# Gate's 4th and 5th inputs in other buffers, eight up pieces ahead of the MLP's first sums, and the last half tile in two pieces

## Chip, cores and metric

The kernel runs on one core of a Trainium2 chip. The metric is the device time of one execution in microseconds (us). Engines are named as in the profile: PE (TensorE, matrix products and transposes), DVE (VectorE), ACT (ScalarE), POOL (GpSimd) and SP (SyncE, which only issues transfers, DMAs, here). SBUF is the memory on the chip that all of them share, PSUM the banks that products are summed in.

## The reference

One layer of a bidirectional encoder on a sequence of 2048 rows of 1024 numbers (float32): attention with two groups of heads, an MLP, and a gated embedding, each behind a norm and added to the row.

```python
u = rmsnorm(h, g_pre_mix); proj = u @ w_in
mix = concat([rmsnorm(windowed_gqa_sink(...)), rmsnorm(dilated_mixture(...))]) @ w_o
h = h + rmsnorm(mix, g_post_mix)
v_ = rmsnorm(h, g_pre_mlp)
a = relu(v_ @ w_up)                       # w_up: 1024 x 4096
h = h + rmsnorm((a * a) @ w_down, g_post_mlp)
gate = sigmoid(h @ w_ple_gate + b_ple_gate)
h = h + rmsnorm(gate * (p @ w_ple_proj), g_post_ple)
```

## The kernel before, in words

Every float32 product is made of three products of parts: each operand is split into a high part (a rounded copy, made by ACT) and a low part (the difference, made by DVE), and hi times hi, lo times hi and hi times lo are summed in PSUM. A "piece" below is such a group of three products for one slice of 128 of the summed index, with 512 columns each. The names end in h and l for the two parts: `uph`, `upl` of the up weights, `dnh`, `dnl` of the down weights, `ah`, `al` of the MLP's inner values, `hh_`, `hl_` of a gate tile.

The stages follow one another: projection, attention, out projection and norms (32 half tiles, counted by `s`, up to 1258 us of the profile), MLP (1258 to 2614 us), gate (2614 us to the end).

**MLP.** The loop over `n` has 32 rounds (two halves of the rows, 16 groups of columns of the up weights each). A round makes the sums of one group, in 28 "downs" of three products each (`down`, L1284, products at L1293, into PSUM tiles `psd` and `psy`), and beside them the up products of the next round, 32 pieces (`up`, L1265). One of these 32 pieces stands behind most of the downs. The down products are arranged so that seven are made where eight would be needed, of sums and differences of operands, which POOL makes (`combo`, L1137, results `tmp`). Steps that other engines must do are put into a queue by `later(dt, step)`; `tick()`, called once behind each down, issues those that are due. So the order on PE, ACT, DVE, POOL and SP in this stage is written out by the code, and each engine runs its own instructions in that order.

The first round is special: its first down needs `al` of the first inner values, which stand behind the last norms of the stage before on DVE (`norm2`, L1099). `FIRST` is a table that puts some of the first round's steps at other ticks. In the first round of each half, `piece` copies sums of `psd` and `psy` by ACT, into the accumulators `acc` (L1296), and for the second of the seven products into `dmp` (L1299), which POOL then adds; a `psy` tile is free for the next down when its copy has been made. There are two `psy` tiles.

**Up weights.** `up_weights(ahead)` (L1143) issues the load of one weight group into `upraw` (L1147, one buffer), and queues four steps: high part of its first half `ahead` ticks later (ACT, L1153), low part (DVE, L1156), and the same of the second half. The buffer is free when the last low part is made. In the out-projection stage it is called at `s` of 8, 15 and 28.

**Gate.** Sixteen tiles `t` of 128 rows, `d_item(t)` in three steps: load `h` and `pl` (`s1`, L1498 and L1500), transpose `h` on PE (L146) and split it (`s2`, L128 and L129), and products, sigmoid, norm and store (`s3`, from L1515 on). For t of 0 to 2 the transposes and splits, and for 0 and 1 the products, are made in the MLP's last round, from `heads`. The loads `h2` share three buffers, and the `h` of a tile is added to its result at the very end, so the buffer of tile 0 is free for tile 3 only when tile 0's result is made. SP's order here comes from a scheduler.

**Last tile.** The last tile's two halves of 512 columns are worked off in turn: bias (L1527), sigmoid (L1528), times `pl` (L1529), square sum (L1531, ACT), times `gp` (L1532); then the two square sums are added (`mt`, L1540), 1 over the root is made by POOL (`rstd_of`), and the result is written (L1543).

Of the kernel before, what the change touches and what calls it, by code (L numbers as in the profile page):

```python
# [12 lines left out]
F32 = mybir.dt.float32  # L13
# [6 lines left out]
D = 1024  # L20
# [39 lines left out]
def layer(ctx, tc, a, out):  # L60
# [354 lines left out]
    def tick():  # L415
        while clock[0] in todo:
            for fn in todo.pop(clock[0]):
                fn()
        clock[0] += 1
# [698 lines left out]
    E_ = 32  # L1118
    FIRST = {6: 17, 14: 21, 15: 22, 16: 23, 17: 24, 18: 21, 20: 23, 24: 25}
    halves_ = []  # L1120
    for n, t in enumerate(c_order):
# [241 lines left out]
    for s in range(E_):  # L1363
        n, hf = s // 2, s % 2
        if hf == 0:
            c_norm(n)
        halves_[n](hf)
        if s in (8, 15, 28):
            up_weights(6 if s == 28 else 3)
        if s == E_ - 1:  # L1370
            prepare(0, x, xs, ws, (-17, FIRST))
        if s >= 19:
            next(u0)
            done += 1
        tick()
    wopx.close()
    stage.close()
    with ExitStack() as st:
# [24 lines left out]
        def gate_load():  # L1403
            for t in range(3):
                h = ru.tile([128, D], F32, name="h0", tag="upraw") if t == 2 else vr.tile([128, D], F32, name="h0", tag="vraw")
                sp.dma_start(h, hd[128 * t : 128 * t + 128, :])
                heads[t] = [h]

        def gate_turn(t, g):
# [28 lines left out]
        for n in range(32):  # L1438
# [19 lines left out]
            if n < 31:  # L1458
                x, xs, ws = {}, [], []
                work = (xs, ws)  # L1460
                prepare((n + 1) % 16, x, xs, ws)
                u = up((n + 1) // 16, (n + 1) % 16, x)
            if n == 30:
                later(20, gate_load)
            if n == 31:
                u = gate_first()
            done = 0
            for m in range(28):
                next(d)
                if n == 31 and m < 4:  # L1470
                    gate_turn(m // 2, m % 2)
                while u and done < ((m + 1) * 32 // 28 if n < 31 else (m - 3) * 32 // 24):
                    next(u)
                    done += 1
                if u and m == 27:
                    run(u)
                feed_up()
                tick()
# [14 lines left out]
        def d_item(t):  # L1493
            box = {}

            def s1():
                h = hp.tile([128, D], F32, name="h2", tag="h2", bufs=3)
                sp.dma_start(h, hd[128 * t : 128 * t + 128, :])  # L1498
                pl = hp.tile([128, D], F32, name="pl", tag="pl", bufs=3)
# [15 lines left out]
            def s3():  # L1515
                y = hp.tile([128, D], F32, name="y", tag="y")
                if t == 15:
                    ms = sml.tile([128, 2], F32, name="ms2", tag="ms2")
                for hf in range(2):
# [3 lines left out]
                    else:  # L1523
                        ps = psm.tile([128, 512], F32, name="psm", tag="psm")
                        mm3(ps, 8, lambda k: box["hh"][:, k, :], lambda k: box["hl"][:, k, :],
                            lambda k: vt[hf][0][:, k, :], lambda k: vt[hf][1][:, k, :])
                    dve.tensor_add(y[:, cs], ps, bb[:, cs])  # L1527
                    act.activation(y[:, cs], y[:, cs], AF.Sigmoid)  # L1528
                    dve.tensor_mul(y[:, cs], y[:, cs], box["pl"][:, cs])  # L1529
                    if t == 15:  # L1530
                        act.activation(box["pl"][:, cs], y[:, cs], AF.Square, scale=1.0 / 32.0, accum_out=ms[:, hf : hf + 1])  # L1531
                        dve.tensor_mul(y[:, cs], y[:, cs], gp[:, cs])  # L1532
                if t < 15:
# [4 lines left out]
                else:  # L1538
                    mt = sml.tile([128, 1], F32, name="mt", tag="mt")
                    dve.tensor_add(mt, ms[:, 0:1], ms[:, 1:2])  # L1540
                    r = rstd_of(mt)
                    for cs in (slice(0, 512), slice(512, 1024)):
# [40 lines left out]
```

## Time and profile before

| what | before |
|---|---|
| three runs | 2798.73, 2804.01, 2804.07 us; median 2804.01 |
| the profiled execution | 2803.37 us |
| its span, first to last instruction | 2801.6 us |
| granted TensorE clock, mean over the span | 0.987 of full speed |
| PE busy | 2716.6 us, 97% of the span |

The time of an execution is 1.77 us more than its span. PE is busy in nearly all slices of the profile, so what can be won lies in the stretches where PE waits, or runs at a lower granted clock. [...]

### The profile page before, as it was taken

To read this page: it belongs to the slowest core of one execution; us is meant where nothing else is said; L and a number is where in the kernel's file an instruction comes from. 1 tells how busy PE (TensorE), PEld (TensorE's weight loads), DVE (VectorE), ACT (ScalarE), POOL (GpSimd) and SP (SyncE) were. 2 spreads that over 40 slices of the span, in tenths; PEclk is the share of its full clock that TensorE was granted. 3 is DMA by queue.
4 is the path that set the end of the run, shared out by engine and by line. 5 is a ranking of instruction groups with operands and counts; after the bars stand their busy time and mean duration, and the time that the engine had idled before them with its cause. 6 is when DMAs were issued, how large, how long until landed. Compare 5 with 4: busy or idle time off the path is not lost.

```text
span 2801.6 us, 38950 instructions
## 1 busy us (share of the span) xinstructions
PE 2716.6 (97%) x13952; PEld 2129.1 (76%) x13952; DVE 1755.1 (63%) x3420; ACT 1273.3 (45%) x2944; POOL 933.1 (33%) x950
## 2 busy tenths in 40 slices
PE   7999999999999999999999999999999999999898
PEld 6878866666677677777888888888888888887687
DVE  4210244456666563776787787777677778786665
ACT  4321345566565554555444444445444444443332
POOL 3000033331322211435345345345345345344220
PEclk9999999999999899999999999999999999999999
DMA  6232252325534325773222122235223223333553
GB/s 178 83 116 81 97 158 74 112 78 141 134 85 127 72 95 169 268 249 98 79 72 75 61 76 72 68 124 195 102 69 104 91 73 112 102 94 150 195 197 104
DMA packets 247873, 324.39 MB, mean 116 GB/s; under 512 B 19904, under 2 KB 175552, under 8 KB 245280
## 3 DMA queue, kind: packets, MB, share of 16 engines
q1 hardware_dynamic: 220544, 281.73, 32.0%
q10 hardware_dynamic: 27136, 40.18, 4.0%
q8 instruction: 110, 1.80, 0.3%
q14 instruction: 83, 0.68, 0.1%
HBM read 227.16 MB, written 102.04 MB: 118 GB/s over the span
## 4 chain that ended last, share of the span: by engine, by line
PE 53%; DVE 1%; ACT 1%; issue 0%; DMA 0%; POOL 0%; DVEq 0%; POOLq 0%; ACTq 0%
PE psd L1293 13%; PE psy L1293 10%; PE psu L174 9%; PE psu L175 9%; PE psu L173 8%; PE psm L137 2%; PE psm L138 2%; PE psm L139 2%; PE pst L146 0%; ACT dmp L1341 0%; ACT y L1528 0%; DMA out_dram<-y 0%; DVE dnl L1132 0%; DVE y L1536 0%; DVE hl L1419 0%
## 5 line engine op out<-in xcount | busy, mean ns | idle before, releaser
L1302 DVE TENSOR_TENSOR acc<-acc,psd 128x512 f32<-128x512 f32 x488 | 332.6, 685 | 190.7 <-PE psd L1293 185.2
L174 PE MATMUL psu<-vt,uph 128*128 128x512 f32 x1024 | 407.4, 398 | 0.0
L175 PE MATMUL psu<-vt,upl 128*128 128x512 f32 x1024 | 404.7, 395 | 0.0
L173 PE MATMUL psu<-vt,uph 128*128 128x512 f32 x1024 | 401.8, 392 | 0.0
L1137 POOL TENSOR_TENSOR tmp<-rl 128x512 f32<-128x512 f32 x64 | 84.2, 1316 | 673.8 <-ACT rl L1281 673.2
L768 ACT ACTIVATE e<-e,tm 128x256 f32<-128x256 f32 (+1 forms) x384 | 176.6, 461 | 120.3 <-DVE tm L765 118.7
L174 PEld LDWEIGHTS psu<-vt,uph 128*128 128x128 f32 x1024 | 192.3, 188 | 48.1
L173 PEld LDWEIGHTS psu<-vt,uph 128*128 128x128 f32 x1024 | 192.6, 188 | 45.0
L175 PEld LDWEIGHTS psu<-vt,upl 128*128 128x128 f32 x1024 | 192.1, 188 | 43.6
L1302 DVE TENSOR_TENSOR acc<-acc,psy 128x512 f32<-128x512 f32 x248 | 170.1, 686 | 86.3 <-PE psy L1293 76.3
L1280 ACT ACTIVATE rl<-psu 128x512 f32<-128x512 f32 x128 | 76.4, 597 | 305.7 <-PE psu L175 305.7
L1300 POOL TENSOR_TENSOR acc<-acc,dmp 128x512 f32<-128x512 f32 x128 | 191.3, 1506 | 57.9 <-DVE al L1132 31.5
L1293 PE MATMUL psd<-dnh,al 128*128 128x512 f32 x512 | 204.0, 398 | 4.8 <-DVE al L1132 4.8
L133 DVE SCALAR_TENSOR_TENSOR wc<-wraw,pre_mix_t,wc 128x128 fp32r<-128x128 f32 x176 | 58.4, 379 | 234.9 <-ACT wc L132 234.9
L1293 PE MATMUL psd<-dnh,ah 128*128 128x512 f32 x512 | 202.1, 395 | 1.9 <-ACT ah L1131 1.9
L1293 PE MATMUL psd<-dnl,ah 128*128 128x512 f32 x512 | 201.4, 393 | 0.0
L765 DVE CUSTOM_DVE_ANT_0 e<-ps_s,b 128x256 f32<-128x256 f32 (+1 forms) x384 | 122.7, 375 | 105.0 <-PE ps_s L752 104.7
L173 PE MATMUL psm<-uhi,wc 128*128 128x512 f32 x448 | 181.7, 410 | 0.3 <-ACT uhi L128 0.3
L174 PE MATMUL psm<-ulo,wc 128*128 128x512 f32 x448 | 177.9, 397 | 0.0
L175 PE MATMUL psm<-uhi,wc 128*128 128x512 f32 x448 | 177.6, 396 | 0.0
L1293 PE MATMUL psy<-dnh,al 128*128 128x512 f32 x384 | 152.5, 397 | 0.0
L1293 PE MATMUL psy<-dnh,ah 128*128 128x512 f32 x384 | 151.1, 394 | 0.0
(697 smaller groups left out, 6254.0 us busy)
## 6 DMA issues: line engine op xcount, KB each, us to landing
upraw<-in_w_up_dram SPq DMA_DIRECT2D x64, 512.0 KB, 4.7
dnraw<-in_w_down_dram SPq DMA_DIRECT2D x64, 512.0 KB, 5.1
h<-hd SPq DMA_DIRECT2D x35, 512.0 KB, 4.7
xt<-in_x_dram SPq DMA_DIRECT2D x32, 512.0 KB, 4.3
wraw<-in_w_in_dram SPq DMA_DIRECT2D x26, 512.0 KB, 4.2
qkd<-sgt ACTq DMA_DIRECT2D x52, 256.0 KB, 2.3
mad<-sgt ACTq DMA_DIRECT2D x32, 256.0 KB, 2.0
acc<-mad SPq DMA_DIRECT2D x16, 512.0 KB, 6.5
```

Source lines behind the costliest of these rows:

```text
L133: dve.scalar_tensor_tensor(lo, src, g, hi.bitcast(F32), op0=ALU.mult, op1=ALU.subtract)
L137: pe.matmul(ps, lh(k), rh(k), start=k == 0, stop=False)
L173: pe.matmul(ps, lh(k), rh(k), start=k == 0, stop=False)
L174: pe.matmul(ps, lh(k), rl(k), start=False, stop=False)
L175: pe.matmul(ps, ll(k), rh(k), start=False, stop=k == n - 1)
L765: dve.tensor_tensor_reduce(ej, box["ps"][hh][:, 256 * jj : 256 * jj + w], bs[hh] if p == 2 else bs[hh][:, var], scale=1.0, scalar=3.0e38, ...
L768: act.activation(ej, ej, AF.Exp, bias=tm, scale=-1.0, accum_out=box["dn"][p][:, i : i + 1])
L1137: pool.tensor_tensor(t, x, y, op=op)
L1280: act.activation(rl, ps, AF.Relu)
L1293: pe.matmul(ps, l[:, js], r, start=start and m == 0, stop=m == 2, skip_group_check=True)
L1300: pool.tensor_tensor(t, t, d, op=ALU.add)
L1302: dve.tensor_add(t, t, ps)
```

## The change

There are three edits. First, the third call of `up_weights` in the out-projection stage moves from `s` of 28 to 24, with its steps 8 instead of 6 ticks behind it; in the first MLP round eight up pieces (24 products) and their ticks stand ahead of the first down, the other 24 pieces are spread over the 28 downs, and seven of the first round's steps come four ticks later. Second, the gate's `h` of tiles 3 and 4 are loaded in the last MLP round into the two buffers that held raw down weights (`wraw`), so that tile 5 is the first to wait for a buffer of tile 0. Third, the last half tile is worked off in two pieces of 256 columns, and 1 over the root is asked for ahead of the products with `gp`.

```diff
@@ -1117,6 +1117,7 @@
 
     E_ = 32
     FIRST = {6: 17, 14: 21, 15: 22, 16: 23, 17: 24, 18: 21, 20: 23, 24: 25}
+    FIRST.update({dt: dt + 4 for dt in (32, 33, 36, 38, 40, 41, 46)})
     halves_ = []
     for n, t in enumerate(c_order):
         steps, half = c_tile(n, t, c_box[n])
@@ -1365,8 +1366,8 @@
         if hf == 0:
             c_norm(n)
         halves_[n](hf)
-        if s in (8, 15, 28):
-            up_weights(6 if s == 28 else 3)
+        if s in (8, 15, 24):
+            up_weights(8 if s == 24 else 3)
         if s == E_ - 1:
             prepare(0, x, xs, ws, (-17, FIRST))
         if s >= 19:
@@ -1405,6 +1406,11 @@
                 h = ru.tile([128, D], F32, name="h0", tag="upraw") if t == 2 else vr.tile([128, D], F32, name="h0", tag="vraw")
                 sp.dma_start(h, hd[128 * t : 128 * t + 128, :])
                 heads[t] = [h]
+
+        def gate_late(t):
+            h = raws.tile([128, D], F32, name="h0", tag="wraw")
+            sp.dma_start(h, hd[128 * t : 128 * t + 128, :])
+            heads[t] = [h]
 
         def gate_turn(t, g):
             pl = fus[t]
@@ -1458,18 +1464,25 @@
             if n < 31:
                 x, xs, ws = {}, [], []
                 work = (xs, ws)
+                u = up((n + 1) // 16, (n + 1) % 16, x)
+                ahead = 8 if n == 0 else 0
+                for _ in range(ahead // 2):
+                    next(u)
+                    next(u)
+                    tick()
                 prepare((n + 1) % 16, x, xs, ws)
-                u = up((n + 1) // 16, (n + 1) % 16, x)
             if n == 30:
                 later(20, gate_load)
             if n == 31:
                 u = gate_first()
-            done = 0
+                for t in (3, 4):
+                    later(14, lambda t=t: gate_late(t))
+            done = ahead
             for m in range(28):
                 next(d)
                 if n == 31 and m < 4:
                     gate_turn(m // 2, m % 2)
-                while u and done < ((m + 1) * 32 // 28 if n < 31 else (m - 3) * 32 // 24):
+                while u and done < (ahead + (m + 1) * (32 - ahead) // 28 if n < 31 else (m - 3) * 32 // 24):
                     next(u)
                     done += 1
                 if u and m == 27:
@@ -1494,8 +1507,11 @@
             box = {}
 
             def s1():
-                h = hp.tile([128, D], F32, name="h2", tag="h2", bufs=3)
-                sp.dma_start(h, hd[128 * t : 128 * t + 128, :])
+                if t in (3, 4):
+                    h = heads[t][0]
+                else:
+                    h = hp.tile([128, D], F32, name="h2", tag="h2", bufs=3)
+                    sp.dma_start(h, hd[128 * t : 128 * t + 128, :])
                 pl = hp.tile([128, D], F32, name="pl", tag="pl", bufs=3)
                 sp.dma_start(pl, pled[128 * t : 128 * t + 128, :])
                 if t == 1:
@@ -1515,7 +1531,7 @@
             def s3():
                 y = hp.tile([128, D], F32, name="y", tag="y")
                 if t == 15:
-                    ms = sml.tile([128, 2], F32, name="ms2", tag="ms2")
+                    ms = sml.tile([128, 3], F32, name="ms3", tag="ms3")
                 for hf in range(2):
                     cs = slice(512 * hf, 512 * hf + 512)
                     if t < 2:
@@ -1524,21 +1540,31 @@
                         ps = psm.tile([128, 512], F32, name="psm", tag="psm")
                         mm3(ps, 8, lambda k: box["hh"][:, k, :], lambda k: box["hl"][:, k, :],
                             lambda k: vt[hf][0][:, k, :], lambda k: vt[hf][1][:, k, :])
-                    dve.tensor_add(y[:, cs], ps, bb[:, cs])
-                    act.activation(y[:, cs], y[:, cs], AF.Sigmoid)
-                    dve.tensor_mul(y[:, cs], y[:, cs], box["pl"][:, cs])
+                    parts = [cs] if t < 15 or hf == 0 else [slice(512, 768), slice(768, 1024)]
+                    for c in parts:
+                        dve.tensor_add(y[:, c], ps[:, c.start - 512 * hf : c.stop - 512 * hf], bb[:, c])
+                        act.activation(y[:, c], y[:, c], AF.Sigmoid)
+                    for i, c in enumerate(parts):
+                        dve.tensor_mul(y[:, c], y[:, c], box["pl"][:, c])
+                        if t == 15:
+                            act.activation(box["pl"][:, c], y[:, c], AF.Square, scale=1.0 / 32.0,
+                                           accum_out=ms[:, hf + i : hf + i + 1])
                     if t == 15:
-                        act.activation(box["pl"][:, cs], y[:, cs], AF.Square, scale=1.0 / 32.0, accum_out=ms[:, hf : hf + 1])
-                        dve.tensor_mul(y[:, cs], y[:, cs], gp[:, cs])
+                        if hf:
+                            mt = sml.tile([128, 1], F32, name="mt", tag="mt")
+                            dve.tensor_add(mt, ms[:, 0:1], ms[:, 1:2])
+                            v = sml.tile([128, 1], F32, name="var", tag="var")
+                            dve.scalar_tensor_tensor(v, ms[:, 2:3], EPS, mt, op0=ALU.add, op1=ALU.add)
+                            r = sml.tile([128, 1], F32, name="rstd", tag="rstd")
+                            pool.tensor_tensor(r, v, nhalf, op=ALU.pow)
+                        for c in parts:
+                            dve.tensor_mul(y[:, c], y[:, c], gp[:, c])
                 if t < 15:
                     r = rms(y, box["pl"])
                     dve.scalar_tensor_tensor(y, y, r, gp, op0=ALU.mult, op1=ALU.mult)
                     dve.tensor_add(y, y, box["h"])
                     sp.dma_start(out_v[t], y)
                 else:
-                    mt = sml.tile([128, 1], F32, name="mt", tag="mt")
-                    dve.tensor_add(mt, ms[:, 0:1], ms[:, 1:2])
-                    r = rstd_of(mt)
                     for cs in (slice(0, 512), slice(512, 1024)):
                         dve.scalar_tensor_tensor(y[:, cs], y[:, cs], r, box["h"][:, cs], op0=ALU.mult, op1=ALU.add)
                         sp.dma_start(out_v[t][:, cs], y[:, cs])
```

What this moves is shown on three engines. Line numbers of the code after the change are up to 26 higher than before.

DVE at the end of the out-projection stage, from the norm of the 15th tile to the first low parts of the MLP (`upl` of the up weights of group 2, `dnl` of the first down weights, `al` of the first inner values), before:

```order
L1091 TENSOR_TENSOR acc_11914<-acc_11914,xt 128x1024
L1156 TENSOR_TENSOR upl<-upraw,uph 128x512
L1132 TENSOR_TENSOR dnl<-dnraw,dnh 128x512
L1099 SCALAR_TENSOR_TENSOR acc_12165<-acc_11914,rstd,gm 128x1024
L1156 TENSOR_TENSOR upl<-upraw,uph 128x512
L1132 TENSOR_TENSOR dnl<-dnraw,dnh 128x512
L1132 TENSOR_TENSOR al<-rl,ah 128x512
L1132 TENSOR_TENSOR dnl<-tmp,dnh 128x512
L1132 TENSOR_TENSOR al<-rl,ah 128x512
L1156 TENSOR_TENSOR upl<-upraw,uph 128x512
L1132 TENSOR_TENSOR dnl<-tmp,dnh 128x512
L1156 TENSOR_TENSOR upl<-upraw,uph 128x512
```

and after:

```order
L1091 TENSOR_TENSOR acc_11914<-acc_11914,xt 128x1024
L1157 TENSOR_TENSOR upl<-upraw,uph 128x512
L1133 TENSOR_TENSOR dnl<-dnraw,dnh 128x512
L1099 SCALAR_TENSOR_TENSOR acc_12168<-acc_11914,rstd,gm 128x1024
L1133 TENSOR_TENSOR dnl<-dnraw,dnh 128x512
L1133 TENSOR_TENSOR al<-rl,ah 128x512
L1133 TENSOR_TENSOR dnl<-tmp,dnh 128x512
L1133 TENSOR_TENSOR al<-rl,ah 128x512
L1157 TENSOR_TENSOR upl<-upraw,uph 128x512 x2
L1133 TENSOR_TENSOR dnl<-tmp,dnh 128x512
L1133 TENSOR_TENSOR al<-tmp,ah 128x512
L1157 TENSOR_TENSOR upl<-upraw,uph 128x512
```

The last `upl` of group 2 has moved from behind the last norm to ahead of it; the two `upl` of group 3 now stand together behind the second `al`.

ACT in the first MLP round, around the first copies of `psy` into `dmp` (`acc` is an accumulator of the MLP), before:

```order
L1296 ACTIVATE acc_12240<-psd 128x512
L1112 ACTIVATE vs<-pst 128x512
L1296 ACTIVATE acc_12241<-psd 128x512
L1131 ACTIVATE ah<-tmp 128x512
L1299 ACTIVATE dmp<-psy 128x512
L1131 ACTIVATE dnh<-dnraw 128x512
L1299 ACTIVATE dmp<-psy 128x512
L1131 ACTIVATE ah<-tmp 128x512
L1299 ACTIVATE dmp<-psy 128x512
L1153 ACTIVATE uph<-upraw 128x512
L1299 ACTIVATE dmp<-psy 128x512
```

and after:

```order
L1297 ACTIVATE acc_12240<-psd 128x512
L1281 ACTIVATE rl<-psu 128x512
L1282 ACTIVATE rl<-rl 128x512
L1297 ACTIVATE acc_12241<-psd 128x512
L1297 ACTIVATE acc_12242<-psd 128x512
L1154 ACTIVATE uph<-upraw 128x512
L1300 ACTIVATE dmp<-psy 128x512
L1132 ACTIVATE dnh<-dnraw 128x512
L1300 ACTIVATE dmp<-psy 128x512
L1132 ACTIVATE ah<-tmp 128x512
L1154 ACTIVATE uph<-upraw 128x512
L1300 ACTIVATE dmp<-psy 128x512 x2
```

The first `uph` of group 4 stood behind three of the `dmp`; it now stands ahead of the first.

SP at the start of the gate (`splg` is the split gate weights, `bb` and `gp` the bias and the norm's weights, `h` numbered by its buffer's use, the L1335 and L1354 of the MLP's last norms), before:

```order
L1172 DMA vt_23064<-splg_96 128x1024
L1502 DMA bb<-in_b_ple_gate_dram 128x1024
L1503 DMA gp<-in_g_post_ple_dram 128x1024
L1498 DMA h_23430<-hd 128x1024
L1500 DMA pl<-pled 128x1024
L1498 DMA h_23434<-hd 128x1024
...
L1500 DMA pl<-pled 128x1024 x2
L1537 DMA out_dram<-y 128x1024
L1498 DMA h_23476<-hd 128x1024
L1354 DMA hd<-h_23460 128x1024
```

and after:

```order
L1173 DMA vt_23064<-splg_96 128x1024
L1412 DMA h_23268<-hd 128x1024
L1412 DMA h_23270<-hd 128x1024
L1518 DMA bb<-in_b_ple_gate_dram 128x1024
L1519 DMA gp<-in_g_post_ple_dram 128x1024
L1514 DMA h_23434<-hd 128x1024
...
L1516 DMA pl<-pled 128x1024 x2
L1566 DMA out_dram<-y 128x1024
L1514 DMA h_23614<-hd 128x1024
L1355 DMA hd<-h_23464 128x1024
```

The loads of tiles 3 and 4 (`h_23268`, `h_23270`) now stand ahead of `bb`; the load behind the first store, which was tile 3's (`h_23476`), is now tile 5's (`h_23614`). On PE the eight transposes of tile 3, which stood behind tile 2's 48 products, now stand behind 22 of them.

## Rows read from the trace of the kernel before

**Rows 1.** The page, busy us (share of the span) and instructions of PE.
```profile
PE 2716.6 (97%) x13952; PEld 2129.1 (76%) x13952; DVE 1755.1 (63%) x3420; ACT 1273.3 (45%) x2944; POOL 933.1 (33%) x950
```

**Rows 2.** Waits of PE: by what; us in total, times, longest us.
```profile
PE pst L146 <- DMA h<-hd: 10.5, 1, 10.5
...
PE psd L1293 <- DVE al L1132: 4.8, 1, 4.8
```

**Rows 3.** Timeline of PE, MLP's first sums: start us, us, instruction, [idle before <-releaser].
```profile
1259.89 0.50 PE L1293 MATMUL psd<-dnh,ah 128*128 128x512 f32 x1 [1.87 <-ACT ah L1131]
...
1265.43 0.79 PE L1293 MATMUL psd<-dnh,al 128*128 128x512 f32 x1 [4.83 <-DVE al L1132]
...
1269.01 0.63 PE L174 MATMUL psu<-vt,uph 128*128 128x512 f32 x1
1269.44 0.45 PE L175 MATMUL psu<-vt,upl 128*128 128x512 f32 x1
```

**Rows 4.** Timeline of DVE, the same place.
```profile
1258.08 2.28 DVE L1099 SCALAR_TENSOR_TENSOR acc<-acc,rstd,gm 128x1024 f32<-128x1024 f32 x1 [1.01 <-POOL rstd L1054]
1260.28 1.75 DVE L1156 TENSOR_TENSOR upl<-upraw,uph 128x512 fp32r<-128x512 f32 x1
...
1263.63 1.75 DVE L1132 TENSOR_TENSOR al<-rl,ah 128x512 fp32r<-128x512 f32 x1
...
1266.98 0.68 DVE L1132 TENSOR_TENSOR al<-rl,ah 128x512 fp32r<-128x512 f32 x1
```

**Rows 5.** Timeline of SP, the load of up weights group 3.
```profile
1262.06 0.37 SPq L1147 DMA_DIRECT2D upraw<-in_w_up_dram  x1
```

**Rows 6.** Timeline of ACT in the first MLP round.
```profile
1266.58 0.63 ACT L1153 ACTIVATE uph<-upraw 128x512 fp32r<-128x512 f32 x1 [3.59 <-DMA upraw<-in_w_up_dram]
...
1274.35 0.60 ACT L1299 ACTIVATE dmp<-psy 128x512 f32<-128x512 f32 x1 [0.33 <-ACT ah L1131]
```

**Rows 7.** Timeline of PE, a short wait in the attention stage.
```profile
635.97 1.65 PE L752 MATMUL ps_s<-bk,qn 64*128 64x256 f32 x5 [2.11 <-DVE tm L765]
```

**Rows 8.** Windows: stretch, its length; busy of five engines, PE clock, DMA share, GB/s.
```profile
635.00:640.00 5.00, 4.03 (x18) 2.61 (x18) 3.81 (x20) 3.77 (x17) 0.00 (x0) 0.50 0.88 326
2640.00:2650.00 10.00, 10.00 (x45) 8.34 (x45) 6.54 (x10) 2.23 (x5) 3.98 (x3) 0.91 0.97 344
```

**Rows 9.** Timeline of PE in the gate, from tile 3's transposes on.
```profile
2636.09 1.94 PE L146 MATMUL pst<-ident,h 128*128 128x128 f32 x8 [10.51 <-DMA h<-hd]
2638.35 0.79 PE L137 MATMUL psm<-vt,hh__23516 128*128 128x512 f32 x1 [0.31 <-ACT hh__23516 L128]
...
2641.50 0.49 PE L139 MATMUL psm<-vt,hl__23517 128*128 128x512 f32 x1
...
2645.48 1.03 PE L146 MATMUL pst<-ident,h 128*128 128x128 f32 x8
```

**Rows 10.** Timeline of SP in the gate.
```profile
2629.62 0.34 SPq L1537 DMA_DIRECT2D out_dram<-y  x1
2630.01 0.42 SPq L1498 DMA_DIRECT2D h<-hd  x1
```

**Rows 11.** The chain that ended last, its end: start us, us, what.
```profile
2792.10 0.23 PE psm L138
...
2792.59 0.70 DVE y L1527
...
2795.46 0.69 DVE y L1532
...
2796.26 0.16 DVE var L117
...
2797.14 0.75 DVE y L1543
```

**Rows 12.** Groups of instructions of 256 columns: xcount | busy us, mean ns of one | idle before.
```profile
L129 DVE TENSOR_TENSOR ol__10336<-pt,oh__10335 128x256 fp32r<-128x256 f32 x1 | 0.4, 426 | 1.9 <-ACT oh__10335 L128 1.9
L128 ACT ACTIVATE oh__10373<-pt 128x256 fp32r<-128x256 f32 x1 | 0.4, 387 | 0.4 <-PE pt L146 0.4
```

## Prediction

> **What bounds the kernel now.** I read the page first. It shows PE busy for 97% of the span [rows 1]; time can only come from PE's idle or slowed stretches, or from what lies behind its last product. The list of PE's waits says where the idle stretches are: the longest single one, 10.5 us, is for the gate's `h`, and one of 4.8 us at the MLP's first sums is for `al` [rows 2]; a smaller one for `ah` stands just ahead of it [rows 3]. The three edits aim at these and at the tail, so I then read the timelines of each engine there, and the chain of waits at the end.
>
> At the first sums PE waits 1.87 us ahead of the first product and 4.83 us ahead of the third, and then runs its products some 0.45 us apart up to 1269.44 [rows 3]. DVE shows why `al` is late: it comes behind the last norm (1258.08), an `upl` and a `dnl`, and starts only at 1263.63 [rows 4]. In the gate PE waits 10.51 us for tile 3's `h` and then makes transposes in 1.94 us that take 1.03 us later, and products 0.45 us apart (seven steps from 2638.35 to 2641.50) [rows 9]. That load was issued at 2630.01, right behind tile 0's store at 2629.62, which had to come first because the buffer was tile 0's [rows 10].
>
> **What the first edit removes.** The two waits are 6.70 us. Behind them PE took nine steps from 1265.43 to 1269.44, 4.01 us [rows 3]; at the 0.23 us of a product late in the kernel [rows 11] they would take 2.07, so the slow stretch costs 1.9. Together 8.6 us. This is only won if the operands are ready when PE comes to them. PE's up products end at about 1258.0 (1259.89 less 1.87 [rows 3]). Now 24 more products (24 x 0.23 = 5.5 us) and two sets of four transposes (some 0.4 us each, by the 1.03 us of eight in the gate [rows 9], whose end overlaps the next product) follow, to about 1264.3. On DVE one `upl` moves from behind the last norm to the 1.01 us of idle time ahead of it [rows 4], where an `upl` without company takes about 0.68 us, so the norm isn't delayed. Behind the norm stand one `dnl` and then `al`: start 1261.96, end 1263.7, each step being 1.68 us as from 1260.28 to 1263.63, two steps [rows 4]. Need is at 1264.7 (the third product). It fits with 1.0 us to spare. `ah` starts on ACT no later than before, as ACT's order ahead of it loses an `uph` and gains none. Both waits go: **+8.6 us**.
>
> **What the first edit adds.** ACT's order now has the first `uph` of group 4 ahead of the first `dmp`, where three `dmp` stood ahead of it. ACT works in order, so all `dmp` wait for group 4's load. That load needs the `upraw` buffer, free when DVE has made both `upl` of group 3, which now stand behind the second `al`. Counting on from 1263.63: `dnl`, `al`, `upl`, `upl`, at 1.68 us while POOL's `combo` runs (to about 1267) and some 0.7 afterwards, gives about 1269.1. From issue to the `uph` that waits for it, group 3's load took 4.52 us (1262.06 [rows 5] to 1266.58 [rows 6]). So `uph` at 1273.6, 0.5 us later `dmp`, which takes 0.60 us [rows 6]: the first `psy` tile is free at about 1274.8. PE wants it for the third `psy` down, 33 products behind 1264.3, at 1264.3 + 33 x 0.23 = 1271.9. A new wait of **2.9 us**. A wait of this size has a price behind it: a wait of 2.11 us in the attention stage [rows 7] is followed by a stretch at clock 0.50 [rows 8]. I add the same 1.9 us as at the first sums. Bounds: nothing, if the `upl` run fast and the load lands sooner; up to 7 us, if both `upl` take 1.75 us and the load 2 us longer. I take **-4.8 us**, as the rows it is counted from are the very instructions that move. What waits behind `dmp`: POOL's sums of `acc`, and those are not needed until the round's end.
>
> [...]
>
> **What the second edit does.** Tiles 3 and 4 are loaded in the last MLP round. Tile 2's last product ended at 2625.6 (2636.09 less 10.51 [rows 9]); tile 3's transposes now stand ahead of the last 26 of tile 2's 48 products, so PE comes to them at 2625.6 - 26 x 0.23 = 2619.6. From its issue to PE's start tile 3's load took 6.1 us (2630.01 [rows 10], 2636.09 [rows 9]), so any issue before 2613.5 is early enough. The MLP's 1356 us in 32 rounds put the start of the last round near 2572 and its end at 2614; SP has only loads of split gate weights ahead of the two, and the last raw down weights, whose buffers they take, are split at the round's start. Removed: 10.51 + 0.31 us of waits, 1.94 - 1.03 = 0.9 us of slow transposes, 3.15 - 7 x 0.23 = 1.5 us of slow products, all [rows 9]: **+13.2 us**. Tile 3's parts have those 26 products (6.0 us) to be made; ACT and DVE are busy with tiles 0 and 1 there, so a wait of up to 2 us here is possible. What is late next: tile 5's `h`, now the load behind tile 0's store. ACT splits tile 3 ahead of tile 0's last step, so I put this load 1.1 us later than 2630.01 [rows 10], at 2631.1. With the same 6.1 us it lands at 2637.2. PE comes to it behind the end of tile 2's products, now 2625.6 + 0.8 for tile 3's transposes, tile 3's 48 products, 9 of tile 4's, and tile 4's transposes: 2626.4 + 57 x 0.23 + 0.8 = 2640.3. It is 3 us early. The later loads follow their stores at the old distance; by the same count tiles 6 to 8 come 2 to 6 us early.
>
> **What the third edit does.** From the bias sum of the last half to the first result is 2792.59 to 2797.14, 4.55 us, the y times `gp` of 0.69 us among it [rows 11]. In pieces of 256 columns DVE takes 0.43 us and ACT 0.39 [rows 12]. Bias 0 to 0.43 and to 0.86; sigmoids to 0.84 and 1.27; times `pl` to 1.31 and 1.74; squares to 1.72 and 2.15; the first y times `gp` stands on DVE meanwhile; `var` at about 2.28, then 0.88 us for `var` and POOL's power, which is 2797.14 less 2796.26: 3.16. Gain **+1.4 us** (between -0.5, if the pieces don't overlap, and 1.5).
>
> **Sum.** 8.6 - 4.8 + 13.2 + 1.4 = 18.4 us. The profiled execution took 2803.37 us, 1.77 of it outside the span; 0.64 us less than the median of the runs, so I take it as it is: 2803.4 - 18.4 = **2785.0 us**.
>
> **Rivals.** A change of 0.2% (5.6 us) is about what a measurement of this kernel can tell from none.
>
> A, as above, the new wait at `dmp` being there: 2785.0, own range 2781.5 to 2788. Chance 0.54.
>
> B, no new wait: `upl` or the load come sooner, or the buffers last. For it: the wait is the difference of two estimates, each a few steps long. Against: the load's time is a row. 2785.0 - 4.8 = 2780.2. Chance 0.20.
>
> C, the gate's wait comes back in part at tile 5 or later. For it: the DMA share is 0.97 from 2640 to 2650 [rows 8], and the stage now has the same bytes in less time, though two loads earlier. If tile 5's `h` needs 11 us in place of 6.1, PE waits 2 us and slows for some 2, and another such wait follows: 7 us back, 2792.0. Chance 0.16.
>
> D, the tail gains nothing: more and smaller instructions cost what they overlap. 2785.0 + 1.4 + 0.5 = 2786.9. Chance 0.04. [...]
>
> F, the early loads don't come early: `wraw` is freed or SP reaches them too late, past 2613.5, so the 13.2 is not won: 2785.0 + 13.2 = 2798.2. Chance 0.03. Against it: SP's order has them ahead of `bb`.
>
> E, slower: ACT stands at the `uph` of group 4, and everything in order behind it (`dmp`, the next `ah`, the copies of `psd`) with it. To eat all of 18.4 us and 5.6 more, this wait must grow from 2.9 to some 27 us, the load landing near 1298 in place of 1273.6. That would need SP to issue it 24 us late; SP has four small stores ahead of it, whose data PE makes before 1264.3. From a landing near 1292 on, the change is not faster at all. 2809. Chance 0.03.
>
> **Range and chances.** A, B and C hold 0.90. The range goes from 2778 (B with the tail and the gate a little better) to 2792 (C). Faster by over 0.2%, under 2798.4: A to D and half of F, 0.95, less a little for what I don't see, 0.93; within 0.2%: 0.04; slower: 0.03.
>
> **What will show it.** Right: in the waits of PE no `al` at the first sums and no `h` of 10 us; a wait of `psy` or `psd` for a `dmp` near 1272 of about 3 us with a granted clock of 0.5 behind it; ACT's `uph` there waiting for `upraw`; tile 5's transposes without a wait; the end of the chain with pieces of 256 columns, about 3.2 us from bias to result. Wrong: a wait of PE for `h` later in the gate (C), no wait at `dmp` (B), or a wait for `hh_` of tile 3 above 2 us.

## Result and the profile after

The changed kernel took 2787.91 us, the median of four runs (2785.3 to 2790.26), against 2802.79 us of the kernel before in four runs. The ratio is 0.9947, with a 95% interval from 0.9935 to 0.9959: 14.9 us less. The profiled execution took 2785.3 us, its span is 2783.5 us. The prediction was 2785.0 us.

The page's line for PE answers to [rows 1]: 7 us less of busy time, and the same share.

```profile
PE 2709.7 (97%) x13952; PEld 2126.0 (76%) x13952; DVE 1755.0 (63%) x3423; ACT 1272.0 (46%) x2947; POOL 932.5 (33%) x950
```

The waits of PE after (by what; us in total, times, longest us), those at the places of the change:

```profile
PE psy L1294 <- ACT dmp L1300: 2.9, 1, 2.9
PE pst L146 <- DMA h<-hd: 2.9, 1, 2.9
```

The three waits of [rows 2] and [rows 3] are gone: nothing for `al` or `ah` at the first sums, and no 10.5 us for `h`. Two new ones have come, of 2.9 us each: one for a `dmp` of ACT, one for a load of `h`; a third, for a sum of DVE, is 0.2 us here, and 1.5 or 1.6 us in a_again, e1, e5 and e7.

**First sums.** PE's timeline there (columns as in rows 3):

```profile
1263.24 0.39 PE L1294 MATMUL psd<-dnh,ah 128*128 128x512 f32 x1
1263.47 0.40 PE L1294 MATMUL psd<-dnl,ah 128*128 128x512 f32 x1
1263.70 0.40 PE L1294 MATMUL psd<-dnh,al 128*128 128x512 f32 x1
...
1274.00 0.50 PE L1294 MATMUL psy<-dnh,ah 128*128 128x512 f32 x1 [2.92 <-ACT dmp L1300]
...
1275.28 0.63 PE L175 MATMUL psu<-vt,upl 128*128 128x512 f32 x1
...
1278.68 0.40 PE L174 MATMUL psu<-vt,uph 128*128 128x512 f32 x1
...
1289.97 0.50 PE L1294 MATMUL psy<-dnh,ah 128*128 128x512 f32 x1 [0.20 <-DVE acc L1303]
```

The three products of the first down follow each other without a gap. The wait comes some eleven us later, at the third `psy`, and soon behind it, from 1275.28 to 1278.68, the products stand 0.43 us apart (eight steps in 3.40 us). ACT and SP say why there is a wait. ACT:

```profile
1268.42 1.07 ACT L1297 ACTIVATE acc<-psd 128x512 f32<-128x512 f32 x2
1272.83 0.63 ACT L1154 ACTIVATE uph<-upraw 128x512 fp32r<-128x512 f32 x1 [3.34 <-DMA upraw<-in_w_up_dram]
1273.37 0.58 ACT L1300 ACTIVATE dmp<-psy 128x512 f32<-128x512 f32 x1
```

and SP, the load of group 4 of the up weights:

```profile
1268.40 0.37 SPq L1148 DMA_DIRECT2D upraw<-in_w_up_dram  x1
```

ACT waits 3.34 us at the `uph` of group 4, with the first `dmp` behind it, though PE made the three products for that `dmp` from 1268.12 on. Group 4's load was issued at 1268.40, when DVE had made both `upl` of group 3.

**Gate.** PE's transposes of tiles 5 to 8:

```profile
2634.12 1.03 PE L146 MATMUL pst<-ident,h 128*128 128x128 f32 x8
...
2655.64 1.03 PE L146 MATMUL pst<-ident,h 128*128 128x128 f32 x8
2675.69 1.06 PE L146 MATMUL pst<-ident,h 128*128 128x128 f32 x8 [2.90 <-DMA h<-hd]
```

Tiles 3 to 7 are transposed without a wait, where tile 3 had 10.51 us [rows 9]; tile 8 waits. SP shows its load (L1514) right behind a store, tile 5's, at 2670.53:

```profile
2670.53 0.34 SPq L1566 DMA_DIRECT2D out_dram<-y  x1
2670.93 0.43 SPq L1514 DMA_DIRECT2D h<-hd  x1
```

**Tail.** The end of the chain:

```profile
2775.83 0.44 DVE y L1545
2776.29 0.42 ACT y L1546
2776.74 0.44 DVE y L1548
2777.20 0.52 ACT pl L1550 x2
2778.42 0.63 POOLq L1605
2779.08 0.75 DVE y L1569
```

From the bias sum to the first result is now 2775.83 to 2779.08, 3.25 us, against 4.55 [rows 11].

**Where the time came from.** Three marks cut each trace: the start of the last norm on DVE (the 2.3 us `acc` of L1099), the gate's first product on PE (the first `psm` of L137), and the last product of the kernel (the last of L139). The lengths between them, and the start of the first, in us, of every profile of this study:

| kernel | last norm starts | to the gate | to the last product | to the end |
|---|---|---|---|---|
| before | 1258.08 | 1356.1 | 178.0 | 9.4 |
| after | 1256.96 | 1351.2 | 167.2 | 8.1 |
| after, again (a_again) | 1261.84 | 1351.0 | 168.7 | 8.1 |
| e1, first edit | 1259.43 | 1351.8 | 178.5 | 9.4 |
| e2, second edit | 1259.27 | 1356.5 | 169.0 | 9.5 |
| e3, third edit | 1256.46 | 1355.7 | 177.0 | 8.1 |
| e4, `uph` later | 1264.36 | 1347.4 | 168.3 | 8.1 |
| e5, five buffers | 1260.69 | 1350.9 | 164.1 | 8.1 |
| e6, both | 1257.84 | 1346.3 | 164.1 | 8.1 |
| e7, tail in one piece | 1255.43 | 1352.0 | 167.4 | 8.9 |
| e8, weights late | 1262.79 | 1352.8 | 166.9 | 8.1 |
| e9, weights early alone | 1262.78 | 1355.3 | 178.5 | 9.4 |

Between the two profiled executions the span fell by 18.1 us: 4.9 in the MLP, 10.8 in the gate, 1.3 in the tail, and 1.1 in the stages ahead, where the code differs only by the moved call of `up_weights`. Each row is one profile. Up to the gate the lengths spread by some 1 us over the three kernels without any of the first edit (before, e2, e3), and by as much over the five profiles with exactly that edit (after, a_again, e1, e5, e7); in the gate, by some 1.5 us without the second edit and by 2.1 us with it and three buffers going round.

### The profile page after: what moved, and what is told of

It is laid out like the page before. It is cut to its first block, busy times and chain, and to the rows that moved or that the text cites. A ratio compares the mean times of both kernels' runs of the same rounds, so it can differ in the third digit from the quotient of the medians.

```text
span 2783.5 us, 38953 instructions
## 1 busy us (share of the span) xinstructions
PE 2709.7 (97%) x13952; PEld 2126.0 (76%) x13952; DVE 1755.0 (63%) x3423; ACT 1272.0 (46%) x2947; POOL 932.5 (33%) x950
## 4 chain that ended last, share of the span: by engine, by line
PE 53%; DVE 1%; DMA 0%; issue 0%; ACT 0%; POOL 0%; DVEq 0%; POOLq 0%; SPq 0%; ACTq 0%
PE psd L1294 13%; PE psy L1294 10%; PE psu L175 9%; PE psu L173 8%; PE psu L174 8%; PE psm L139 2%; PE psm L138 2%; PE psm L137 2%; PE pst L146 0%; DVE dnl L1133 0%; DMA h<-hd 0%; DVE y L1565 0%; DMA upraw<-in_w_up_dram 0%; DVE al L1133 0%; DVE upl L1157 0%
## 5 line engine op out<-in xcount | busy, mean ns | idle before, releaser
L1303 DVE TENSOR_TENSOR acc<-acc,psd 128x512 f32<-128x512 f32 x488 | 332.3, 685 | 189.2 <-PE psd L1294 183.6
L1303 DVE TENSOR_TENSOR acc<-acc,psy 128x512 f32<-128x512 f32 x248 | 170.1, 686 | 84.2 <-PE psy L1294 74.0
L175 PE MATMUL psm<-uhi,wc 128*128 128x512 f32 x448 | 178.0, 397 | 0.0
L1294 PE MATMUL psy<-dnl,ah 128*128 128x512 f32 x384 | 152.6, 397 | 0.0
```

The lines of the kernel that those rows point to most:

```text
L175: pe.matmul(ps, ll(k), rh(k), start=False, stop=k == n - 1)
L1294: pe.matmul(ps, l[:, js], r, start=start and m == 0, stop=m == 2, skip_group_check=True)
L1303: dve.tensor_add(t, t, ps)
```

## Experiments

**Each edit alone.** Three kernels with the diff above cut to one of its edits, timed in five rounds on one chip beside the kernel before.

To the kernel before, the core of each:

```diff
e1
+    FIRST.update({dt: dt + 4 for dt in (32, 33, 36, 38, 40, 41, 46)})
...
+            up_weights(8 if s == 24 else 3)
...
+                ahead = 8 if n == 0 else 0
e2
+                    later(14, lambda t=t: gate_late(t))
...
+                if t in (3, 4):
+                    h = heads[t][0]
e3
+                    parts = [cs] if t < 15 or hf == 0 else [slice(512, 768), slice(768, 1024)]
```

> Only the first edit (up weights earlier, eight up pieces ahead, table). Mine: the two waits of 6.7 us at the first sums and the 1.9 us of slow products go, and a new wait for the dmp of about 2.9 us with some 1.9 us of slow products behind it comes, as in the trace of the changed kernel: 4 to 5 us less than before. Rival: the gain seen between the two profiles up to the gate is mostly the 1 us by which the attention stage happened to end earlier, and the new wait eats the rest: 0 to 2 us less.

Measured: ratio 0.999 (0.998 to 0.9999), 2.8 us less; the interval reaches from 0.3 to 5.6 us. The times alone don't tell the theories apart. The trace does: the stage up to the gate is 1351.8 us, 4.3 less than before, and the other two parts are as before. The wait for the `dmp` is there, and so is one for a sum of DVE:

```profile
PE psy L1294 <- ACT dmp L1300: 2.8, 1, 2.8
...
PE psy L1294 <- DVE acc L1303: 1.6, 1, 1.6
```

> Only the second edit (gate inputs of tiles 3 and 4 early). Mine: 13.2 us less the 2.9 us for which PE now waits for tile 8's h: 10 to 11 us less than before, with that wait in the trace. Rival: tile 8's wait was a matter of one execution, or of the earlier edit's shift: 13 us less and no wait for h.

Measured: ratio 0.9965 (0.9951 to 0.9979), 9.8 us less; the gate takes 169.0 us, 8.9 less than before, a little under the 10 to 11 that I expected: the clock fell to 0.50 behind the wait (last section). The wait for tile 8's `h` is in this trace as well, without the other edits:

```profile
PE pst L146 <- DMA h<-hd: 3.0, 1, 3.0
```

So it belongs to the second edit and is no matter of one execution: all five other profiles with the second edit and three buffers going round (after, a_again, e4, e7, e8) have it, with 2.4 to 3.0 us.

> Only the third edit (last half tile in two pieces). Mine: 1.3 us less than before, which the times can hardly tell; the chain from the bias sum to the result is 3.2 to 3.3 us where before has 4.55. Rival (fixed cost of an instruction): 4.5 us or more in the chain, no gain.

Measured: ratio 1.0001 (0.9989 to 1.0013), which tells nothing of 1.3 us. The chain has the step from 2789.59 (bias) to 2792.84 (result), 3.25 us, to the hundredth that of the changed kernel, and the tail is 8.1 us long:

```profile
2789.59 0.44 DVE y L1529
...
2792.84 0.75 DVE y L1553
```

**The tail in one piece.**

```diff
-                    parts = [cs] if t < 15 or hf == 0 else [slice(512, 768), slice(768, 1024)]
+                    parts = [cs]
-                            dve.tensor_add(mt, ms[:, 0:1], ms[:, 1:2])
-                            dve.scalar_tensor_tensor(v, ms[:, 2:3], EPS, mt, op0=ALU.add, op1=ALU.add)
+                            dve.scalar_tensor_tensor(v, ms[:, 1:2], EPS, ms[:, 0:1], op0=ALU.add, op1=ALU.add)
```

> The changed kernel with the last half tile in one piece of 512 columns, 1 over the root still asked for ahead of the products with gp, the two square sums added in one instruction. Mine: the chain from the bias sum to the result is about 3.8 us: 0.7 us of the third edit's gain is the product with gp leaving the chain, and 0.5 us the overlap of the pieces. Rival: the pieces cost what they overlap, and the chain is 3.2 to 3.3 us as with them.

Measured, the chain:

```profile
2775.29 0.70 DVE y L1545
...
2779.36 0.75 DVE y L1567
```

2775.29 to 2779.36 is 4.07 us, where I had 3.8. The pieces are worth 0.8 us (4.07 against 3.25), and 0.5 us (4.55 against 4.07) came otherwise: I had the two parts the wrong way round. The product with `gp` and the sum `mt` had 0.80 us of the chain before (2795.46 to 2796.26 [rows 11]), and both have left it here. Some of that came back on POOL: its power took 0.55 us before, with DVE idle from `var` to the result, and 0.86 us here, where the product with `gp` stands behind `var` in DVE's order:

```profile
2796.56 0.55 POOL L119 TENSOR_TENSOR rstd<-var,nhalf 128x1 f32<-128x1 f32 x1 [10.70 <-DVE var L117]
```

```profile
2778.46 0.86 POOL L1557 TENSOR_TENSOR rstd<-var,nhalf 128x1 f32<-128x1 f32 x1 [9.90 <-DVE var L1555]
```

In the changed kernel it starts at 2778.45, the second of the two smaller products ends at 2778.64, and it takes 0.60 us.

**Taking the two new waits away.** Two small edits to the changed kernel, one for each of its new waits, alone and together, timed beside the changed kernel and the one before on one chip.

> The changed kernel again, to stand beside the three that follow on the same chip. Both theories: a ratio to before near 0.9947.

Measured: the ratio is 0.9944 (0.9932 to 0.9957).

The first gives group 4 of the up weights seven ticks in place of three, so that its `uph` stands behind the four `dmp` in ACT's order:

```diff
         if ups["next"] < 64 and ups["live"] < 3 and not ups["busy"]:
-            up_weights()
+            up_weights(7 if ups["next"] == 4 else 3)
```

> The changed kernel with the steps of up weights group 4 four ticks later, so that ACT makes the first four dmp ahead of group 4's first uph. Mine: PE's wait of 2.9 us for the dmp goes, and the slow products behind it: 4 to 5 us less than the changed kernel. Rival: the load is late for someone in any order, so the wait only moves (to the up products of the second round, or to DVE's al behind the upl): 0 to 1 us less.

Measured: ratio 0.9925 (0.9912 to 0.9939). The stage up to the gate is 1347.4 us, 3.6 to 3.8 less than in the changed kernel's two profiles, the wait for the `dmp` is gone, and no wait has come in its place in the MLP's first 40 us. I had 4 to 5 us; in the medians it is 5.0 (2783.97 against 2788.99). ACT's first `dmp` now only waits for its sums:

```profile
1277.20 0.60 ACT L1300 ACTIVATE dmp<-psy 128x512 f32<-128x512 f32 x1 [0.28 <-PE psy L1294]
```

The rival, that the wait only moves, falls: group 4's weights are first used in the next round.

The second puts the `h` of tiles 8, 9, 13 and 14 into the two buffers of tiles 3 and 4:

```diff
                 if t in (3, 4):
                     h = heads[t][0]
+                elif t % 5 > 2:
+                    h = raws.tile([128, D], F32, name="h0", tag="wraw")
+                    sp.dma_start(h, hd[128 * t : 128 * t + 128, :])
                 else:
```

> The changed kernel with the h of tiles 8, 9, 13 and 14 also in the two buffers that tiles 3 and 4 had, so that five buffers go round. Mine: tile 8's wait of 2.9 us came of its buffer, free only behind tile 5's store; now its load stands behind tile 3's store, 20 us earlier, and the wait goes: 2.5 to 3 us less than the changed kernel. Rival: DVE is the bound there (9.4 to 9.6 of 10 us busy from 2620 to 2650), so PE waits elsewhere, for PSUM or for the split parts, and the time stays within 1 us.

Measured: ratio 0.9928 (0.9916 to 0.994). The gate takes 164.1 us, 3.1 and 4.6 less than in the changed kernel's two profiles. Tile 8's load is now the one at 2654.33, behind tile 3's store, and PE waits for no `h` at all:

```profile
2653.80 0.43 SPq L1569 DMA_DIRECT2D out_dram<-y  x1
2654.33 0.38 SPq L1514 DMA_DIRECT2D h<-hd  x1
```

DVE's full stretch (below) does not come out as a wait of PE elsewhere, so the rival falls.

> Both of these (group 4 later, five buffers). Mine: the two gains add up, 7 to 8 us less than the changed kernel. Rival: no more than the larger of the two.

Measured: ratio 0.9915 (0.9901 to 0.9928), median 2778.57 us, against 2788.99 of the changed kernel beside it: 10.4 us less, where I had 7 to 8. In the stages, 1346.3 and 164.1 us, it is 8.0 and 9.3 us less than in the changed kernel's two profiles, about what the two edits give alone, so the rival falls. This is the best version of the study.

**The two halves of the first edit.** The changed kernel with `up_weights` put back (e8), and the kernel before with only `up_weights` moved (e9), one profile each.

```diff
e8 (to the changed kernel)
-        if s in (8, 15, 24):
-            up_weights(8 if s == 24 else 3)
+        if s in (8, 15, 28):
+            up_weights(6 if s == 28 else 3)
e9 (to the kernel before): the same two lines the other way round
```

> The changed kernel with the third call of up_weights back at s of 28 with 6 ticks, the eight pieces still ahead. Mine: the pieces carry most of the first edit. PE waits for the upl behind the last norm, for about 1 us, and al is 1.7 us later but PE comes to it later too: from the last norm on DVE to the gate's first product the stage takes 1 to 2.5 us more than the 1351 to 1352 us of the changed kernel. Rival: the up weights carry it, PE waits 4 us or more at the first sums again, and the stage takes 1355 us or more.

> The kernel before with the third call of up_weights at s of 24 with 8 ticks, and nothing else (no pieces ahead, the table as before). Mine: al comes one upl, 1.7 us, earlier, so the wait for al goes from 4.8 to about 3.1 us, the slow products stay, and from the last norm to the gate's first product the stage takes 1354 to 1355 us where before has 1356. Rival: the up weights carry the first edit, the wait falls under 1 us and the stage takes 1352 us or less.

Measured: e8 1352.8 us up to the gate, 1.6 more than the changed kernel's first profile and 1.8 more than its second; e9 1355.3 us, 0.8 less than before and 0.4 less than the shortest of the three kernels without the edit. By the spreads given under the table these are small differences, but both rivals, 1355 us or more for e8 and 1352 or less for e9, are out: the eight pieces carry most of the edit. But e8's loss is not where I put it: PE doesn't wait for the `upl` at all, and the wait for the `dmp` is longer, since the `upraw` of group 4 is loaded later, 12.64 us behind the start of the last norm where the changed kernel has 11.44.

```profile
PE psy L1294 <- ACT dmp L1300: 3.6, 1, 3.6
```

In e9 `al` still comes 3.7 us late (I had 3.1):

```profile
PE psd L1293 <- DVE al L1132: 3.7, 1, 3.7
```

The move of one `upl` of 1.7 us took 1.1 us off this wait, which is 4.8 us in all three kernels without the first edit. The wait for `ah` ahead of it is 1.4 us, but it is 1.9, 1.5 and 1.2 us in before, e2 and e3, so nothing can be read from it.

## Why the prediction was right, step by step

**The first sums, +8.6.** Right. From the last norm's start to the first down I had 6.2 us (1258.08 to 1264.3), measured 6.28 (1256.96 to 1263.24), and both waits are gone. In e4 and e6, where the new wait is gone too, the stage up to the gate is 8.7 and 9.8 us shorter than before. e8 and e9 show that the pieces do most of it; the early weights help by letting group 4's load start 1.2 us sooner.

**The new wait at `dmp`, -4.8.** The wait itself is right, in place, cause and size: 2.9 us forecast, 2.92 measured (2.4 to 2.8 in four other profiles, 3.6 in e8); from issue to `uph` 4.52 forecast, 4.43 measured. e4 shows the cause by changing ACT's order: 3.6 to 3.8 us come back. The 1.9 us added for slow products is right in size, but in part by luck. Only in the changed kernel's first profile and in e8 did products run slowly behind the wait: 3.40 us for eight steps in the first, where 8 x 0.23 = 1.84 are usual, at a clock of 0.66 from 1275 to 1280, and 2.99 us for seven in e8. In a_again, e1, e5 and e7 the products behind the wait stood 0.23 us apart, and PE waited 1.5 or 1.6 us some 16 us later for a sum of DVE (`acc`, L1303), which reads a `psy`. In a_again:

```profile
1278.88 0.50 PE L1294 MATMUL psy<-dnh,ah 128*128 128x512 f32 x1 [2.40 <-ACT dmp L1300]
...
1294.61 0.50 PE L1294 MATMUL psy<-dnh,ah 128*128 128x512 f32 x1 [1.55 <-DVE acc L1303]
```

Between these two products lie 15.73 us here, 15.97 in the changed kernel's first profile (1274.00 to 1289.97), and 13.94 in e6, which has neither wait. So about 2 us are lost either way, and the slow products cost 0.2 us more than the wait that they nearly filled. The prediction had said of POOL's sums behind `dmp` that they "are not needed until the round's end". Their results are not, but POOL's next `combo` stands behind them, and an `ah` and an `al` behind that (a_again, the three engines):

```profile
1278.90 6.43 POOL L1301 TENSOR_TENSOR acc<-acc,dmp 128x512 f32<-128x512 f32 x4 [6.78 <-ACT dmp L1300]
```

```profile
1287.08 0.63 ACT L1132 ACTIVATE ah<-tmp 128x512 fp32r<-128x512 f32 x1 [0.59 <-POOL tmp L1138]
```

```profile
1287.74 1.10 DVE L1133 TENSOR_TENSOR al<-tmp,ah 128x512 fp32r<-128x512 f32 x1 [1.85 <-ACT ah L1132]
```

In DVE's order the sums of `psy` come behind this `al`. No run holds this chain apart from the first wait: in e4 and e6 both are gone.

With its new waits the whole first edit gives 4.1 to 5.2 us against the stage's length in before (1356.1, and 1350.9 to 1352.0 in after, a_again, e1, e5 and e7), where I had 3.8.

**The two `upl` of group 3.** The prediction took 1.68 us for a low part while POOL's `combo` runs and some 0.7 afterwards. Before, the low parts took 1.75 us each from 1260.28 to 1265.30 [rows 4], with POOL at its `combo`, and the `al` at 1266.98, which started while POOL stood idle, took 0.68 us:

```profile
1264.91 1.60 POOL L1137 TENSOR_TENSOR tmp<-tmp,rl 128x512 f32<-128x512 f32 x1
1267.14 1.66 POOL L1137 TENSOR_TENSOR tmp<-rl 128x512 f32<-128x512 f32 x1 [0.63 <-DVE dnl L1132]
```

After, the two `upl` took 2.38 us together, from 1265.99. POOL was still at a `combo` for the first, up to 1267.22 (DVE's rows, then POOL's):

```profile
1264.28 1.78 DVE L1133 TENSOR_TENSOR al<-rl,ah 128x512 fp32r<-128x512 f32 x1
1265.99 2.38 DVE L1157 TENSOR_TENSOR upl<-upraw,uph 128x512 fp32r<-128x512 f32 x2
```

```profile
1265.48 1.74 POOL L1138 TENSOR_TENSOR tmp<-rl 128x512 f32<-128x512 f32 x1
```

At this place, in both traces, the low parts that started beside POOL's `combo` are the long ones; why, the traces do not show. The sum's own steps, with one `upl` at 1.68 us and one at 0.7, make 1269.4 for the end of both, and not the 1269.1 that stands there; measured it is 1268.4, with the last norm 1.1 us earlier.

**The gate, +13.2.** The wait that was aimed at went as forecast, and the term came out too large: 8.9 to 11.1 us measured (178.0 in the profile of before, 166.9 to 169.0 in those with the second edit and three buffers), since a part of rival C came true in a place that I had counted as safe. It is the first of the prediction's own signs of being wrong, "a wait of PE for `h` later in the gate". The step that failed is "The later loads follow their stores at the old distance; by the same count tiles 6 to 8 come 2 to 6 us early". Tile 5's load, at which I looked for the rival, was early; tile 8's was 2.9 us late. It has to wait for tile 5's store, because three buffers go round and tile 5's is the next, and that store did not move with PE. Before, it came 29.55 us behind tile 5's transposes (2653.89 to 2683.44), after 36.41 (2634.12 to 2670.53). e5 shows the part of the buffer: with tile 8's load behind another store the wait is gone, and in e5 and e6 the gate is 13.9 us shorter than before. So the 13.2 was there, but for tile 8. The load itself was not slow: 4.76 us from its issue to PE's start, where I had counted 6.1.

Why the store fell back can be read in part. First, DVE's windows (columns as in rows 8; DVE is the third figure behind the length). Before, and then after:

```profile
2620.00:2630.00 10.00, 5.59 (x24) 4.14 (x23) 7.20 (x16) 10.00 (x28) 2.54 (x3) 0.90 0.91 340
```

```profile
2620.00:2630.00 10.00, 10.00 (x49) 8.31 (x48) 9.53 (x15) 6.29 (x18) 5.55 (x5) 1.00 0.79 273
2640.00:2650.00 10.00, 10.00 (x50) 8.37 (x49) 9.40 (x12) 2.54 (x6) 6.02 (x4) 1.00 0.79 265
```

While PE waited 10.5 us, up to 2636.09, DVE finished the results of tiles 0 and 1 (their stores stand at 2629.62 and 2635.98) and two of the MLP's last norms. Without that pause it is busy 9.4 to 9.6 of 10 us for 30 us (7.20, 9.44 and 6.54 before), and the stores lag behind the products. Second, a buffer of the results. There are two for `y` (`hp`, `bufs=2`), so tile 5's first bias sum needs the one that tile 3's store frees. In four of the six profiles with tile 8's wait (a_again, e2, e4, e7) the chain that ended last runs to tile 8's load through such a store; in e7:

```profile
2649.67 5.45 DMA out_dram<-y
...
2655.24 0.13 DVE y L1545
...
2655.85 1.28 DVE y L1562
...
2670.32 4.64 DMA h<-hd
```

The store takes 5.4 us to land, where the median of the 15 stores of a whole tile is 2.6 in the profile of before and in the changed kernel's first. DVE stands idle for 2.4 us ahead of the bias sum, and the last steps of tile 4 (from 2655.85), and then those of tile 5, come behind it in DVE's order. In the changed kernel's first profile the same bias sum starts at 2655.85, 5.49 us behind tile 3's store, and a product ends just ahead of it, to which its idle time of 2.33 us is put down. Before, it came 9.7 us behind that store (2660.67, 2670.33). No run tested either reason, by a third buffer for `y` or by taking work off DVE. Bytes, the cause that I named for rival C, stay open too: tile 8's load was not slow, this store was.

**The tail, +1.4.** Right: 1.3 measured in every profile with the whole edit, and e7 splits it, 0.8 for the pieces and 0.5 for what left the chain. Rival D did not come true: a piece takes 0.44 us on DVE where 512 columns take 0.70 [rows 11], which makes the fixed part of an instruction some 0.2 us by an estimate from these two, but the pieces overlap on two engines, and two bias sums of 256 columns, one behind the other, take DVE 0.76 us together.

**The sum.** Forecast 18.4 us. The stages of the edits gave 17.0 between the two profiles, and 1.1 us more came from the stages ahead. In the medians it is 14.9. So the 2785.3 us of the profiled execution beside my 2785.0 is luck in part: the gate gave 2.4 us less than its term between these two profiles, the first edit 1.1 us more, and the stages ahead 1.1 us that no edit was counted on for. Rival A, the likeliest, came true with a part of C; B, D, E and F did not.

## What to carry to other kernels

Before one engine is relieved of a wait, list what the others finish in its shade: a pause of PE is time for DVE, and a store that kept its distance while PE paused may not keep it without the pause (tile 5's: 29.55 us before, 36.41 after). Follow every ring of buffers one full turn, that of the results as well as that of the inputs, and not only to the first load behind the edit. And where engines run in a written order, read what now stands directly behind the instruction that waits for a transfer, and what stands behind that on the next engine; here, moving the steps that wait four ticks later gave back nearly 4 us, and no other wait came.

## What the runs showed of the hardware

The granted clock fell behind some short waits of PE and not behind others of the same length and place. At tile 8's transposes PE waited 3.04 us in e2 and 2.90 us in the changed kernel; in the first 4 us behind the wait (two windows each, columns as in rows 8) the clock fell to 0.50 in the one and stayed at 1.00 in the other. In e2:

```profile
2683.47:2685.47 2.00, 2.00 (x12) 1.75 (x13) 0.48 (x3) 1.86 (x4) 0.85 (x2) 0.82 0.12 43
2685.47:2687.47 2.00, 2.00 (x7) 1.51 (x6) 2.00 (x2) 0.00 (x0) 0.22 (x1) 0.50 0.91 246
```

In the changed kernel:

```profile
2675.69:2677.69 2.00, 2.00 (x13) 1.82 (x14) 0.57 (x3) 1.81 (x4) 0.94 (x2) 1.00 0.13 47
2677.69:2679.69 2.00, 2.00 (x10) 1.63 (x10) 2.00 (x2) 0.00 (x0) 0.13 (x1) 1.00 0.91 246
```

Of the six profiles with this wait, it fell in three (to 0.50 in e2 with 3.04 us, to 0.53 in a_again with 2.78, to 0.52 in e4 with 2.38) and stayed at 1.00 in two (the changed kernel's first with 2.90, e7 with 2.98), so the wait's length doesn't sort them. The gate takes 168.3 to 169.0 us in the three that fell, 167.2 and 167.4 in the two others, and 166.9 in e8, which waited 2.6 us. Behind the wait for the `dmp` the products stood 0.43 us apart for a while in two of six profiles (the changed kernel's first, e8) and 0.23 in the other four. So adding a price for the clock to every such wait, as I did, is right only some of the time, and at the `dmp` another wait stood behind, which the slow products nearly filled.

The clock also differs between profiles in the attention stage, whose code no kernel here changes. Over the twelve profiles the last norm began between 1255.43 (e7) and 1264.36 us (e4), and the mean clock from 600 to 800 us goes with it: 0.97 in e7, 0.94 to 0.96 in the five that began from 1256.96 to 1259.43, 0.92 or 0.93 in the four from 1260.69 to 1262.79, 0.89 in e4; only e3, with 0.93 at 1256.46, doesn't fit. In e4:

```profile
600.00:800.00 200.00, 182.37 (x1377) 134.30 (x1377) 123.17 (x482) 119.56 (x416) 50.88 (x76) 0.89 0.43 118
```

From e7 to e4 the last norm's start moves by 8.9 us, more than half of what the change is worth. That is why the lengths of the stages tell these experiments apart where the whole times don't.
